# Other waiting times for the recorded mixer streams of a two-layer hybrid decoder

## The chip, the cores and the metric

One core of one Trainium2 chip runs the whole kernel as one program. The metric is the device time of one execution in microseconds (us), lower is better. The kernel before takes 931.92 us, the median of three runs (928.59 to 932.09).

## The reference

The reference is a decoder trunk for one sequence of 256 tokens, 1024 wide, in fp32, with two layers. Cut to what matters:

```python
for layer in range(2):
    h = rms_norm(x, norm1_g[layer])
    w_l = w_in[layer]
    ...
    y_sb = merge_heads(stick_breaking_attention(...))
    y_rwkv, v_first = rwkv7_time_mix(...)
    ...
    y_moba = merge_heads(moba_attention(q_m, k_m, ...))
    y_hgrn = hgrn2_mixer(...)
    merged = None
    for n, y_n in enumerate((y_sb, y_rwkv, y_moba, y_hgrn)):
        gate = jax.nn.sigmoid(cols(GATE_OFF + n * D_MODEL, D_MODEL))
        term = gate * (y_n.astype(x.dtype) @ w_branch[layer, n])
        merged = term if merged is None else merged + term
    x = x + merged @ w_out[layer]
    h2 = rms_norm(x, norm2_g[layer])
    x = x + (jax.nn.silu(h2 @ w_ffn_gate[layer]) * (h2 @ w_ffn_up[layer])) @ w_ffn_down[layer]
return rms_norm(x, final_g)
```

Four token mixers work side by side in a layer. RWKV-7 is a recurrence over the tokens; in layer 1 its value rows are first mixed with those of layer 0, `v + (v_first - v) * sigmoid(v0 + (v @ v1) @ v2)`. MoBA is here plain causal attention with a partial rotary on queries and keys, since its block is as long as the sequence.

## The kernel before, in words

A layer has a mixer phase, a merge and an FFN. In all three the large products run on TensorE (PE) in three passes: every fp32 operand is split into a rounded part `hi` and a rest `lo` (`split`, lines 127 to 129: a CAST on ScalarE, ACT, and a subtraction on VectorE, DVE), and `mm3` multiplies hi by hi, hi by lo and lo by hi. Weights come in pieces of 128x1024 (512 KB) over SP's queue into a ring of four `raw` tiles, and their split into a ring of four `hi`/`lo` pairs (pool tags `spl`): a fifth CAST waits for the last matmul of the first weight.

The mixer phase (`phase`, line 1058) writes two kinds of work into one program. *Units* are the projections, the gates (`gate_unit`) and the branch products (`branch_unit`); they are nearly all of PE's work and are drawn from a list. *Streams* are the mixers' inner parts, written as generators: `rwkv` is one; stick-breaking attention (`sba`), MoBA (`moba`) and HGRN (`hgrn`) follow each other in a second, `rest`. `drive` (line 91) keeps an estimate of PE's time, `pe[0]`. When a stream yields a number, it comes next when the estimate has grown by 1.7 times that number of ns; until then units are written. So the yields set where a stream's pieces stand among the units. Behind that the framework's scheduler orders each engine's list once more by its own estimate of what is ready. Every engine then works through its list strictly in order.

What the prediction's steps touch:

- PSUM tiles: `pa` (three buffers, taken in turn) holds the results of the units, `p1` (two) those of RWKV, `p2` (two) those of the attentions and HGRN, `p3` an attention's output. A gate takes two `pa` tiles (t = 0 and 1, the halves of the sequence); they are free again when ACT has read them through a sigmoid (line 1018). HGRN's last projection takes two; each is read on ACT twice (lines 817 and 818), then on DVE (line 819).
- RWKV's triangular inverse. The 16x16 blocks on the diagonal are inverted on DVE in three levels (lines 598 and 601: products and sums of 2x2, 4x4 and 8x8 sub-blocks). ACT's queue then writes the result `yb` to DRAM (line 606, tile `tri`) and reads it back in another layout (line 609, `cb`); DVE masks it (613) and transposes it (623), and PE grows the inverse to 32, 64 and 128 in steps up to line 686. `pair_scores` (line 540) makes the four score tiles and ends in a masked copy on DVE (548).
- MoBA. The rotary of two tiles is two shuffles (987), four products and sums on DVE (988, 990) and two products on GpSimd, POOL (989). Then for each t: scores on PE, mask on DVE (936), row maximum (997, 998), four exponentials on ACT (1001), their scaling on DVE (1003, 1004), transposes on PE (`flip_att`), weighing with the values. Exponential and sigmoid are in different function tables of ACT, and an ACT_TABLE_LOAD stands where one follows the other.
- HGRN ends with transposes of its output (`y_T`) into a `p2` tile, whose split is the left operand of its two branch products.

Of the kernel before, what the change touches and what calls it, by code (L numbers as in the profile page):

```python
# [46 lines left out]
def trunk(ctx, tc, x, w_t, w_n, w_br, w_out, w_gu, w_dn, par, lora, rows, gains, consts, masks, out):  # L47
# [12 lines left out]
    def ps(tag):  # L60
        return psum.tile([128, 512], F32, name=tag, tag=tag, bufs=NB[tag])
# [409 lines left out]
    def rwkv(m, l, yT):  # L471
# [100 lines left out]
        for c in range(2):  # L572
            LK.append(g2d(sb("b1", 1024), 4))
            pair_scores(kh, LK[c], c)
            yield 2400
        yield 500
        nc.vector.tensor_copy(yb.rearrange("p s t -> p (s t)")[:, 1::34],
                              xb.rearrange("p s t -> p (s t)")[:, 1::34])
        tmp = sb("xy", 512)[0:64]
# [1 line left out]
        for lev in range(1, 4):  # L581
            hb = 1 << lev
            nb = 8 // hb

            def blk(q, i, j):
                return bass.AP(tensor=q.tensor, offset=q.offset + i * hb * 16 + j * hb,
                               ap=[q.ap[0], [34 * hb, nb], [16, hb], [1, hb]])

            pr = tmp[:, 0:nb * hb ** 3].rearrange("p (b i c k) -> p b i c k", b=nb, i=hb, c=hb)
            t4 = th[:, 0:nb * hb * hb].rearrange("p (b i c) -> p b i c", b=nb, i=hb)  # L590
            parts = [(slice(None), i) for i in range(hb)] if hb < nb else [(b, slice(None)) for b in range(nb)]
            bc = [64, nb if hb < nb else hb, hb, hb]

            def product(dst, l4, r4):
                r4 = r4.rearrange("p b k c -> p b c k")
                for b, i in parts:
                    r = r4 if hb < nb else r4[:, b, None]
                    nc.vector.tensor_tensor(pr[:, b, i], l4[:, b, i, None].to_broadcast(bc), r.to_broadcast(bc),
                                            op=OP.mult)
                for b, i in parts:  # L600
                    nc.vector.tensor_reduce(dst[:, b, i], pr[:, b, i], axis=AX.X, op=OP.add)

            product(t4, blk(yb, 0, 0), blk(xb, 0, 1))
            product(blk(yb, 0, 1), t4, blk(yb, 1, 1))
        yield 4000
        nc.scalar.dma_start(tri.rearrange("p (s t) -> p s t", s=16), yb)
        yield 2500
        cb = sb("h1", 256)[:, 0:128].rearrange("p (m t) -> p m t", m=8)
        nc.scalar.dma_start(cb, bass.AP(tensor=tri.tensor, offset=tri.offset, ap=[[16, 128], [2048, 8], [1, 16]]))
        yield 2500  # L610
# [75 lines left out]
                (nc.scalar.copy if u else nc.vector.tensor_copy)(Y[c][L64, u::2, H64], g2d(p[hrow(u), 0:128], 2))  # L686
        yield 900

        if l:
            p = ps("p1")  # L690
            for hp in range(2):
                mm(p[0:64, 0:256], v1[:, hp], vx[:, hp], hp == 0, hp == 1)
            vl = sb("h1", 256)
            nc.scalar.copy(vl[0:64], p[0:64, 0:256])
            yield 1000
            sv = lora_up(v2, vl[0:64], P_V0)
            dv = g2d(sb("c1", 512), 2)
            nc.gpsimd.tensor_tensor(dv, g2d(vfirst, 2), vx, op=OP.subtract)
            nc.gpsimd.tensor_tensor(dv, dv, sv, op=OP.mult)
            nc.gpsimd.tensor_tensor(vx, vx, dv, op=OP.add)  # L700
            yield 6000
        p = ps("p1")
        for c in range(2):
            for hp in range(2):
# [32 lines left out]
        for c in range(2):  # L737
# [55 lines left out]
            nc.vector.tensor_tensor(yc, yc, bonus[:, c], op=OP.add)  # L793
            nc.vector.tensor_tensor(yc, yc, g[:, c], op=OP.mult)
            ys.append(yc)
            yield 200
        yield 6000
        yT[1] = y_T(ys, "p1"), pe[0] + 2500

# [25 lines left out]
    def hgrn(m, l, yT):  # L825
# [79 lines left out]
        for t in range(2):  # L905
# [13 lines left out]
            nc.vector.tensor_tensor(y, y, gs[:, t], op=OP.mult)  # L919
            ys.append(y)  # L920
            yield 300
        yield 3500
        yT[3] = y_T(ys, "p2"), pe[0] + 2500

    def scores(q, k, t, mask):
# [57 lines left out]
    def moba(m, v, yT):  # L983
        r = []
        for u in m:
            o = g2d(sb("c2", 512), 2)
            nc.vector.stream_shuffle(o, g2d(u, 2), SWAP)  # L987
            nc.vector.tensor_tensor(o, o, over(sinT, 2), op=OP.mult)
            nc.gpsimd.tensor_tensor(g2d(u, 2), g2d(u, 2), over(cosT, 2), op=OP.mult)
            nc.vector.tensor_tensor(o, o, g2d(u, 2), op=OP.add)  # L990
            r.append(o)
        yield 5000
        po = ps("p3")
        for t in range(2):
            z, n = scores(r[0], r[1], t, cn[:, K_MO:K_MO + 128])
            mxs = sm.tile([128, 4], F32, name="mxs")
            nc.vector.tensor_reduce(mxs, z, axis=AX.X, op=OP.max)
            nc.vector.tensor_scalar(mxs, mxs, -0.125, None, op0=OP.mult)
            den = sm.tile([128, 4], F32, name="den")
            for a in range(4):  # L1000
                nc.scalar.activation(z[:, a], z[:, a], AF.Exp, bias=mxs[:, a:a + 1], scale=0.125,
                                     accum_out=den[:, a:a + 1])
            nc.vector.reciprocal(den, den)
            nc.vector.tensor_tensor(z, z, bcast(den, n), op=OP.mult)
            yield 5000 + 2500 * t
            ts = []
            flip_att(z, t, ts)
            yield 1200
            weigh(po, ts, t, v, 256)
        yT[2] = y_split(po), pe[0] + 2500  # L1010
        yield 500
# [46 lines left out]
    def phase(hr, g, l, ws):  # L1058
# [32 lines left out]
        def rest():  # L1091
            yield from sba(sm_, vv, yT)
            while len(mm_) < 2:
                yield 2000
            yield from moba(mm_, vv, yT)
            while len(hm) < 4:
                yield 2000
            yield from hgrn(hm, l, yT)
# [202 lines left out]
```

## Time and profile before

| | us |
|---|---|
| median of 3 runs (lowest to highest) | 931.92 (928.59 to 932.09) |
| the profiled execution, its own time | 928.13 |
| its span on the core | 926.3 |
| PE busy | 906.9 (98%) |
| DVE busy | 649.1 (70%) |
| ACT busy | 475.4 (51%) |
| POOL busy | 84.5 (9%) |

The profile is of one execution. Its span runs from the first to the last instruction; around it lie 1.8 us that belong to the execution's own time. Busy times are unions over an engine's instructions. Matmuls overlap, and their ends are modelled, so a row's start is surer than its end. In a timeline a row is a run of equal instructions, with the start, the length, and in brackets the idle time of the engine before it with what ended it. PE's loads of weights are an engine of their own there (PEld).

### The profile page before, as it was taken

What the parts mean: (1) busy time and instruction counts of PE and PEld (TensorE: products, weight loads), DVE (VectorE), ACT (ScalarE), POOL (GpSimd) and SP (SyncE); (2) the same over time, 40 slices, a digit from 0 to 9 for tenths busy, and PEclk for the clock granted to TensorE, in tenths of its full rate; (3) what the DMA queues carried; (4) which work ended last, traced back from release to release, by engine and by line L of the source; (5) the groups of instructions that cost most, each with busy time, mean ns of one, the idle gap of its engine ahead of it and who ended that gap; (6) DMA issues with size and microseconds to landing.
All of it is one profiled execution on the core that took longest, in us unless ns stands there. A gap on an engine that the chain in (4) does not pass through costs nothing.

```text
span 926.3 us, 15024 instructions
## 1 busy us (share of the span) xinstructions
PE 906.9 (98%) x5908; PEld 759.1 (82%) x5908; DVE 649.1 (70%) x958; ACT 475.4 (51%) x727; POOL 84.5 (9%) x94
## 2 busy tenths in 40 slices
PE   8999999999999999999999999999999999999996
PEld 5999677778878888888889986777888888888885
DVE  6668877776766666677567778867678566666665
ACT  5564375355535555456445646644455445545453
POOL 3001100333000000000000201032230000000000
PEclk9999999999999999999999999999999999999999
DMA  8644454345864555568435544444367356556551
GB/s 303 218 151 151 127 163 134 95 154 180 263 210 137 182 184 185 183 205 271 154 114 161 159 140 129 151 117 134 119 215 260 112 185 203 192 180 196 182 182 46
DMA packets 50424, 158.11 MB, mean 171 GB/s; under 512 B 9393, under 2 KB 11953, under 8 KB 50354
## 3 DMA queue, kind: packets, MB, share of 16 engines
q1 hardware_dynamic: 43920, 155.71, 52.7%
q10 hardware_dynamic: 6434, 1.45, 0.7%
q8 instruction: 46, 0.75, 0.3%
q14 instruction: 24, 0.20, 0.1%
HBM read 154.91 MB, written 2.23 MB: 170 GB/s over the span
## 4 chain that ended last, share of the span: by engine, by line
PE 86%; DVE 6%; DMA 3%; issue 2%; ACT 2%; POOL 0%; POOLq 0%; ACTq 0%; SPq 0%; DVEq 0%
PE pa L80 61%; PE p L80 23%; DVE lo L129 1%; PE p L89 1%; PE pa L89 1%; DMA h<-flat 1%; DMA tri<-yb 1%; DMA flat<-b 1%; DMA raw<-in_w_out_dram 1%; DVE b L972 1%; ACT hi L128 0%; DVE b L548 0%; DMA xr<-in_x_dram 0%; DVE c L987 0%; DVE b L874 0%
## 5 line engine op out<-in xcount | busy, mean ns | idle before, releaser
L129 DVE TENSOR_TENSOR lo<-raw,hi 128x1024 fp32r<-128x1024 f32 x268 | 330.2, 1237 | 162.7 <-ACT hi L128 159.9
L128 ACT CAST hi<-raw 128x1024 fp32r<-128x1024 f32 x268 | 279.0, 1048 | 237.8 <-PE pa L80 116.8
L80 PE MATMUL pa<-h,hi 128*128 128x256 f32 (+1 forms) x1280 | 277.9, 339 | 0.0
L80 PEld LDWEIGHTS pa<-h,hi 128*128 128x128 f32 x1280 | 215.9, 190 | 24.6 <-issue 2.0
L80 PE MATMUL pa<-hi,h 128*128 128x512 f32 x576 | 193.5, 400 | 2.2 <-DVE p L819 2.2
L80 PE MATMUL pa<-h,lo 128*128 128x256 f32 x960 | 179.9, 283 | 0.0
L80 PEld LDWEIGHTS pa<-h,lo 128*128 128x128 f32 x960 | 148.6, 191 | 7.0 <-issue 0.7
L80 PEld LDWEIGHTS pa<-hi,h 128*128 128x128 f32 x576 | 108.1, 188 | 27.5 <-DVE p L819 3.0
L80 PE MATMUL p<-hi,c 128*128 128x512 f32 (+1 forms) x352 | 113.4, 394 | 0.0
L80 PE MATMUL pa<-lo,h 128*128 128x512 f32 x288 | 112.6, 391 | 0.0
L80 PEld LDWEIGHTS p<-hi,c 128*128 128x128 f32 x352 | 66.1, 189 | 15.2 <-DVE c L129 0.6
L80 PE MATMUL p<-lo,c 128*128 128x512 f32 (+1 forms) x176 | 69.2, 393 | 0.0
L80 PEld LDWEIGHTS pa<-lo,h 128*128 128x128 f32 x288 | 54.2, 188 | 10.1 <-issue 0.3
L263 POOL TENSOR_TENSOR rs<-rs,half 128x1 f32<-128x1 f32 x10 | 6.2, 618 | 477.3 <-DVE rs L262 477.3
L80 PE MATMUL pa<-hi,y 128*128 128x512 f32 x128 | 43.9, 399 | 0.0
L80 PE MATMUL p<-hi,b 128*128 128x512 f32 x128 | 41.5, 397 | 0.6 <-DVE b L129 0.6
L80 PEld LDWEIGHTS p<-lo,c 128*128 128x128 f32 x176 | 33.2, 188 | 6.8
L1040 POOL TENSOR_TENSOR p<-p,gt 128x512 f32<-128x512 f32 x16 | 31.2, 1975 | 54.4 <-DVE gt L1038 54.4
L342 DVE TENSOR_TENSOR gt<-gt,pa 128x256 f32<-128x256 f32 x80 | 33.2, 415 | 0.0
L128 ACT CAST c<-xy 128x512 fp32r<-128x512 f32 x20 | 12.4, 620 | 39.2 <-DVE xy L1143 39.2
L80 PEld LDWEIGHTS pa<-hi,y 128*128 128x128 f32 x128 | 24.0, 188 | 6.4 <-issue 1.0
L341 ACT COPY gt<-pa 128x256 f32<-128x256 f32 x80 | 29.2, 366 | 0.0
(277 smaller groups left out, 939.6 us busy)
## 6 DMA issues: line engine op xcount, KB each, us to landing
raw<-in_w_gu_dram SPq DMA_DIRECT2D x88, 512.0 KB, 3.9
raw<-in_w_n_dram SPq DMA_DIRECT2D x80, 512.0 KB, 3.6
raw<-in_w_dn_dram SPq DMA_DIRECT2D x44, 512.0 KB, 3.6
raw<-in_w_t_dram SPq DMA_DIRECT2D x40, 512.0 KB, 4.1
raw<-in_w_br_dram SPq DMA_DIRECT2D x16, 512.0 KB, 3.6
raw<-in_w_out_dram SPq DMA_DIRECT2D x16, 512.0 KB, 4.4
b<-in_gains_dram SPq DMA_DIRECT2D x4, 512.0 KB, 5.6
flat<-b ACTq DMA_DIRECT2D x4, 256.0 KB, 3.2
```

The costliest lines, as they stand in the source:

```text
L80: nc.tensor.matmul(o, l, r, start=start, stop=stop)
L89: nc.tensor.transpose(o, i, ident)
L128: a = nc.scalar.copy(dst[0], src)
L129: return a, (eng or nc.vector).tensor_tensor(dst[1], src, dst[0], op=OP.subtract)
L263: nc.gpsimd.tensor_tensor(dst, dst, half[:, :dst.shape[-1]], op=OP.pow)
L341: nc.scalar.copy(dst, p[:, 256:512])
L342: nc.vector.tensor_tensor(dst, dst, p[:, 0:256], op=OP.add)
L972: nc.vector.tensor_tensor_scan(kb, kb, reset[t][:, ::-1], 1.0, op0=OP.mult, op1=OP.add)
L1040: e.tensor_tensor(mg[f, t], mg[f, t], g, op=OP.add)
```

## The change

All edits are in the yields and in the order in which the generators issue their work; no operation is added or taken away. (a) Behind the scores of RWKV's second kind the yields become 3000 and 3000 instead of 2400, 2400 and 500. (b) The inverse's three levels yield 100 behind each of their six products, and 1200 behind the last instead of 4000. (c) In layer 1 the mixing of the value rows (two low-rank products on PE, a copy and two sigmoids on ACT, three operations on POOL) is issued between the write of `tri` and its read, instead of behind the whole inverse; in layer 0 a yield of 1000 stands there. (d) The yields behind RWKV's two output halves are 1500 and 200 instead of 200 twice, behind HGRN 4300 instead of 3500, behind MoBA's two softmaxes 6800 and 8300 instead of 5000 and 7500. (e) 5000 more stand ahead of MoBA.

```diff
--- before.py
+++ after.py
@@ -572,8 +572,7 @@
         for c in range(2):
             LK.append(g2d(sb("b1", 1024), 4))
             pair_scores(kh, LK[c], c)
-            yield 2400
-        yield 500
+            yield 3000
         nc.vector.tensor_copy(yb.rearrange("p s t -> p (s t)")[:, 1::34],
                               xb.rearrange("p s t -> p (s t)")[:, 1::34])
         tmp = sb("xy", 512)[0:64]
@@ -601,10 +600,26 @@
                     nc.vector.tensor_reduce(dst[:, b, i], pr[:, b, i], axis=AX.X, op=OP.add)
 
             product(t4, blk(yb, 0, 0), blk(xb, 0, 1))
+            yield 100
             product(blk(yb, 0, 1), t4, blk(yb, 1, 1))
-        yield 4000
+            yield 100
+        yield 1200
         nc.scalar.dma_start(tri.rearrange("p (s t) -> p s t", s=16), yb)
-        yield 2500
+        if l:
+            p = ps("p1")
+            for hp in range(2):
+                mm(p[0:64, 0:256], v1[:, hp], vx[:, hp], hp == 0, hp == 1)
+            vl = sb("h1", 256)
+            nc.scalar.copy(vl[0:64], p[0:64, 0:256])
+            yield 1000
+            sv = lora_up(v2, vl[0:64], P_V0)
+            dv = g2d(sb("c1", 512), 2)
+            nc.gpsimd.tensor_tensor(dv, g2d(vfirst, 2), vx, op=OP.subtract)
+            nc.gpsimd.tensor_tensor(dv, dv, sv, op=OP.mult)
+            nc.gpsimd.tensor_tensor(vx, vx, dv, op=OP.add)
+        else:
+            yield 1000
+        yield 1500
         cb = sb("h1", 256)[:, 0:128].rearrange("p (m t) -> p m t", m=8)
         nc.scalar.dma_start(cb, bass.AP(tensor=tri.tensor, offset=tri.offset, ap=[[16, 128], [2048, 8], [1, 16]]))
         yield 2500
@@ -686,19 +701,6 @@
                 (nc.scalar.copy if u else nc.vector.tensor_copy)(Y[c][L64, u::2, H64], g2d(p[hrow(u), 0:128], 2))
         yield 900
 
-        if l:
-            p = ps("p1")
-            for hp in range(2):
-                mm(p[0:64, 0:256], v1[:, hp], vx[:, hp], hp == 0, hp == 1)
-            vl = sb("h1", 256)
-            nc.scalar.copy(vl[0:64], p[0:64, 0:256])
-            yield 1000
-            sv = lora_up(v2, vl[0:64], P_V0)
-            dv = g2d(sb("c1", 512), 2)
-            nc.gpsimd.tensor_tensor(dv, g2d(vfirst, 2), vx, op=OP.subtract)
-            nc.gpsimd.tensor_tensor(dv, dv, sv, op=OP.mult)
-            nc.gpsimd.tensor_tensor(vx, vx, dv, op=OP.add)
-            yield 6000
         p = ps("p1")
         for c in range(2):
             for hp in range(2):
@@ -793,7 +795,7 @@
             nc.vector.tensor_tensor(yc, yc, bonus[:, c], op=OP.add)
             nc.vector.tensor_tensor(yc, yc, g[:, c], op=OP.mult)
             ys.append(yc)
-            yield 200
+            yield 1500 - 1300 * c
         yield 6000
         yT[1] = y_T(ys, "p1"), pe[0] + 2500
 
@@ -919,7 +921,7 @@
             nc.vector.tensor_tensor(y, y, gs[:, t], op=OP.mult)
             ys.append(y)
             yield 300
-        yield 3500
+        yield 4300
         yT[3] = y_T(ys, "p2"), pe[0] + 2500
 
     def scores(q, k, t, mask):
@@ -1002,7 +1004,7 @@
                                      accum_out=den[:, a:a + 1])
             nc.vector.reciprocal(den, den)
             nc.vector.tensor_tensor(z, z, bcast(den, n), op=OP.mult)
-            yield 5000 + 2500 * t
+            yield 6800 + 1500 * t
             ts = []
             flip_att(z, t, ts)
             yield 1200
@@ -1092,6 +1094,7 @@
             yield from sba(sm_, vv, yT)
             while len(mm_) < 2:
                 yield 2000
+            yield 5000
             yield from moba(mm_, vv, yT)
             while len(hm) < 4:
                 yield 2000
```

What the scheduler makes of it shows in the engines' lists. First DVE in layer 0, around the last level of the inverse: `yb` is the inverse, `xy_1232` or `xy_1235` its products, `c2_1161` or `c2_1226` a rotary tile of MoBA, `lo_` the split of weights, `b1_1178` or `b1_1174` the last score tile of RWKV. Before:

```order
L988 TENSOR_TENSOR c2_1161<-c2_1161,cn_70 128x512
L601 TENSOR_REDUCE yb_124<-xy_1232 64x4x4
L990 TENSOR_TENSOR c2_1161<-c2_1161,p_920 128x512
L601 TENSOR_REDUCE yb_124<-xy_1232 64x4x4
L129 TENSOR_TENSOR lo_1289<-raw_1286,hi_1288 128x1024
L548 COPY_PREDICATED b1_1178<-mk_122,p1_1179 128x2x256
L548 COPY_PREDICATED b1_1178<-mk_122,p1_1180 128x2x256
L598 TENSOR_TENSOR xy_1232<-yb_124,h1_1126 64x512
L601 TENSOR_REDUCE h1_1233<-xy_1232 64x64
L598 TENSOR_TENSOR xy_1232<-h1_1233,yb_124 64x512
L129 TENSOR_TENSOR lo_1307<-raw_1304,hi_1306 128x1024
L601 TENSOR_REDUCE yb_124<-xy_1232 64x8x8
```

Of the change:

```order
L990 TENSOR_TENSOR c2_1226<-c2_1226,cn_70 128x512
L600 TENSOR_REDUCE yb_124<-xy_1235 64x4x4
L992 TENSOR_TENSOR c2_1226<-c2_1226,p_920 128x512
L129 TENSOR_TENSOR lo_1257<-raw_1254,hi_1256 128x1024
L600 TENSOR_REDUCE yb_124<-xy_1235 64x4x4
L597 TENSOR_TENSOR xy_1235<-yb_124,h1_1126 64x512
L548 COPY_PREDICATED b1_1174<-mk_122,p1_1175 128x2x256
L548 COPY_PREDICATED b1_1174<-mk_122,p1_1176 128x2x256
L600 TENSOR_REDUCE h1_1236<-xy_1235 64x64
L597 TENSOR_TENSOR xy_1235<-h1_1236,yb_124 64x512
L129 TENSOR_TENSOR lo_1287<-raw_1284,hi_1286 128x1024
L600 TENSOR_REDUCE yb_124<-xy_1235 64x8x8
```

The rotary's last rows (988 and 990 before, 990 and 992 now) stand in both ahead of the 8x8 level; two masked copies and one split have changed places with their neighbours, and the instructions down to the inverse's last sum are the same.

Next ACT in layer 0, at the first gate behind HGRN's projections: `pa_1284` and `pa_1285` before, `pa_1252` and `pa_1253` now are the gate's two results, `c2_1255` or `c2_1322` MoBA's scores for t = 0, `tri_958` the inverse in DRAM. Before:

```order
L128 CAST hi_1350<-raw_1348 128x1024
L1001 ACT_TABLE_LOAD
L1001 ACTIVATE c2_1255,den_1267<-c2_1255,mxs_1264 128x128 x4
L128 CAST hi_1399<-raw_1397 128x1024
L128 CAST hi_1429<-raw_1427 128x1024
L128 CAST hi_1451<-raw_1449 128x1024
L945 COPY c2_1346<-p2_1341 128x512
L1018 ACT_TABLE_LOAD
L1018 ACTIVATE gt_1360<-pa_1284 128x512
L1018 ACTIVATE gt_1370<-pa_1285 128x512
```

Of the change:

```order
L128 CAST hi_1343<-raw_1341 128x1024
L624 DMA h1_1358<-tri_958 128x8x16
L128 CAST hi_1367<-raw_1365 128x1024
L128 CAST hi_1393<-raw_1391 128x1024
L128 CAST hi_1415<-raw_1413 128x1024
L1020 ACTIVATE gt_1353<-pa_1252 128x512
L1003 ACT_TABLE_LOAD
L1003 ACTIVATE c2_1322,den_1334<-c2_1322,mxs_1331 128x128 x4
L1020 ACT_TABLE_LOAD
L1020 ACTIVATE gt_1363<-pa_1253 128x512
L128 CAST hi_1437<-raw_1435 128x1024
```

The four exponentials and their two table loads stood ahead of both gate sigmoids; now they stand between the first and the second. The read of `tri` has moved behind a CAST (before it stood ahead of line 817 for t = 1).

Last PE in layer 0, at the transposes of HGRN's output (`p2_2354` or `p2_2457`); their split is `y_2359` and `y_2360` before, `y_2462` and `y_2463` now. Before:

```order
L89 MATMUL p2_2354<-cn_70,h2_2269 128x128
L89 MATMUL p2_2354<-cn_70,h2_2298 128x128
L89 MATMUL p2_2354<-cn_70,h2_2269 128x128
L89 MATMUL p2_2354<-cn_70,h2_2298 128x128
L80 MATMUL pa_2238<-hi_2339,h4_140 128x512
L80 MATMUL pa_2238<-lo_2340,h4_140 128x512
L80 MATMUL pa_2238<-hi_2339,h4_140 128x512
L80 MATMUL pa_2368<-hi_2372,h4_139 128x512
L80 MATMUL pa_2368<-lo_2373,h4_139 128x512
L80 MATMUL pa_2368<-hi_2372,h4_139 128x512 x2
```

Of the change:

```order
L80 MATMUL pa_2311<-hi_2417,h4_140 128x512
L89 MATMUL p2_2457<-cn_70,h2_2377 128x128
L89 MATMUL p2_2457<-cn_70,h2_2406 128x128
L89 MATMUL p2_2457<-cn_70,h2_2377 128x128
L89 MATMUL p2_2457<-cn_70,h2_2406 128x128
L80 MATMUL pa_2472<-hi_2468,y_2462 128x512
L80 MATMUL pa_2472<-lo_2469,y_2462 128x512
L80 MATMUL pa_2481<-hi_2468,y_2462 128x512
L80 MATMUL pa_2481<-lo_2469,y_2462 128x512
L80 MATMUL pa_2472<-hi_2468,y_2463 128x512
L80 MATMUL pa_2472<-hi_2468,y_2462 128x512
L80 MATMUL pa_2472<-lo_2469,y_2462 128x512
```

Behind the transposes followed the rest of one gate and a whole further gate before the branch products with `y_2359`; now the branch products with `y_2462` follow at once. Layer 1 reads the same at this place.

## Rows read from the trace of the kernel before

**Rows 1.** The page: PE's line of part 1 (busy us, share of the span, instructions), and the granted clock of the 40 slices of part 2 in tenths.

```profile
PE 906.9 (98%) x5908; PEld 759.1 (82%) x5908; DVE 649.1 (70%) x958; ACT 475.4 (51%) x727; POOL 84.5 (9%) x94
...
PEclk9999999999999999999999999999999999999999
```

**Rows 2.** The waits of PE over the whole span: engine, tile and line that waited, what for; us in total, times, longest.

```profile
PE p L89 <- DVE c L1004: 2.5, 2, 1.3
PE pa L80 <- DVE p L819: 2.2, 2, 1.1
PE p L80 <- DVE b L548: 1.6, 2, 0.8
...
PE p L80 <- DVE h L767: 1.0, 1, 1.0
```

**Rows 3.** The timeline of PE in layer 0's mixer phase: start us, us, engine, line, operation, out<-in, shapes, count, and in brackets the idle time before and what ended it. From the row at 111.98 to the idle time ahead of the one at 120.39 PE works off thirty matmuls of 512 columns.

```profile
93.30 1.13 PE L80 MATMUL p<-b,c 64*128 64x256 f32 x8
...
99.22 1.75 PE L80 MATMUL p<-b,c 64*128 64x256 f32 x8 [0.77 <-DVE b L548]
...
107.24 0.71 PE L80 MATMUL p<-c,c 64*128 64x128 f32 x8
107.88 0.50 PE L80 MATMUL pa<-hi,h 128*128 128x512 f32 x1
...
111.98 0.50 PE L80 MATMUL pa<-hi,h 128*128 128x512 f32 x1 [1.07 <-DVE p L819]
...
120.39 0.63 PE L89 MATMUL p<-cn,c 128*128 128x128 f32 x4 [1.32 <-DVE c L1004]
```

**Rows 4.** The timeline of DVE over the same stretch.

```profile
97.19 0.72 DVE L987 STREAM_SHUFFLE c<-p 128x512 f32<-128x512 f32 x1
...
98.46 1.32 DVE L548 COPY_PREDICATED b<-mk,p 128x512 f32<-128x512 uint8 x2
...
108.44 1.20 DVE L129 TENSOR_TENSOR lo<-raw,hi 128x1024 fp32r<-128x1024 f32 x1
109.58 0.67 DVE L601 TENSOR_REDUCE yb<-xy 64x64 f32<-64x512 f32 x1
...
111.50 0.42 DVE L819 TENSOR_TENSOR p<-p,pa 128x256 f32<-128x256 f32 x1
111.84 0.75 DVE L936 TENSOR_TENSOR c<-p,cn 128x256 f32<-128x256 f32 x2
112.62 0.69 DVE L997 TENSOR_REDUCE mxs<-c 128x4 f32<-128x512 f32 x1
113.34 0.17 DVE L998 TENSOR_SCALAR mxs<-mxs 128x4 f32<-128x4 f32 x1
...
116.97 1.28 DVE L613 TENSOR_TENSOR xy<-h,mk 128x512 f32<-128x512 f32 x2
118.17 1.29 DVE L623 STREAM_TRANSPOSE xy<-xy 128x512 f32<-128x512 f32 x2
```

**Rows 5.** The timeline of ACT over the same stretch; ACTq is its queue, on which it issues DMAs.

```profile
110.28 0.49 ACTq L606 DMA_DIRECT2D tri<-yb  x1
110.81 0.37 ACT L817 COPY p<-pa 128x256 f32<-128x256 f32 x1 [3.77 <-DVE yb L601]
111.08 0.39 ACT L818 ACTIVATE p<-pa 128x256 f32<-128x256 f32 x1
113.61 0.38 ACTq L609 DMA_DIRECT2D h<-tri  x1
...
115.64 1.28 ACT L1001 ACT_TABLE_LOAD   x1
116.94 0.40 ACT L1001 ACTIVATE c<-c,mxs 128x128 f32<-128x128 f32 x1
...
118.50 2.93 ACT L128 CAST hi<-raw 128x1024 fp32r<-128x1024 f32 x3
```

**Rows 6.** The DMAs that write or read `tri`, all four of them: from issue to landing.

```profile
DMA to landing us min/median/max: 2.8/2.9/3.3
```

**Rows 7.** Groups of ACT by line with forms kept apart: count, busy us, mean ns of one, idle time before.

```profile
L1018 ACT ACTIVATE gt<-pa 128x512 f32<-128x512 f32 x32 | 18.5, 596 | 8.7 <-PE pa L80 8.4
...
L1001 ACT ACTIVATE b<-b,mxs 128x256 f32<-128x256 f32 x8 | 4.0, 498 | 0.0
```

**Rows 8.** The timeline of layer 0 behind the scores for t = 1: DVE's maximum and scaling of MoBA, and PE's 32-wide step of the inverse.

```profile
127.78 1.21 DVE L997 TENSOR_REDUCE mxs<-b 128x4 f32<-128x1024 f32 x1
...
133.36 1.22 DVE L1004 TENSOR_TENSOR b<-b,den 128x1024 f32<-128x1024 f32 x1
...
145.36 0.69 PE L80 MATMUL p<-h,b 32*32 32x32 f32 x32
```

**Rows 9.** The timeline at the end of layer 0's HGRN: its transposes on PE and the split of their result on ACT and DVE.

```profile
208.25 0.60 PE L89 MATMUL p<-cn,h 128*128 128x128 f32 x4
...
208.88 0.59 ACT L128 CAST y<-p 128x512 fp32r<-128x512 f32 x1 [0.46 <-PE p L89]
...
209.50 0.69 DVE L129 TENSOR_TENSOR y<-p,y 128x512 fp32r<-128x512 f32 x1 [0.79 <-ACT y L128]
```

**Rows 10.** The timeline of PE in layer 1, at the two places that answer to 111.98 and 120.39 in layer 0.

```profile
565.75 0.50 PE L80 MATMUL pa<-hi,h 128*128 128x512 f32 x1 [1.09 <-DVE p L819]
...
574.00 0.63 PE L89 MATMUL p<-cn,c 128*128 128x128 f32 x4 [1.16 <-DVE c L1004]
```

## The prediction

> **What bounds the kernel now.** I read the page first: PE is busy for 98% of the span and the granted clock is at its upper level, 2.4 GHz, in every slice [rows 1]. So other engines cost time only where they let PE wait, and the change leaves PE's work as it is. The table of PE's waits comes next: the mixer phases of both layers lose 2.5 us to the scaling of MoBA's probabilities, 2.2 us to HGRN's line 819, 1.6 us to RWKV's masked copy and 1.0 us to line 767 [rows 2]. The timeline shows where: one stall each in either layer, and for the copy more than the idle time says, because the same eight matmuls take 1.13 us at 93.30 and 1.75 us at 99.22, a hidden 0.62 us [rows 3]. What could be won by moving instructions is thus about 7.3 + 1.2 = 8.5 us, 0.9%; the question is which stalls go and what is late next. The orders of the engines say more on this than the yields do.
>
> **The inverse and the stall at line 819.** PE needs HGRN's first result buffer back at 111.98. It comes back when DVE ends line 819 at 111.92, which started at 111.50, and that waited for ACT's lines 817 and 818 at 110.81 and 111.08 [rows 3 to 5]. ACT was late because the write of `tri` stands ahead of them in its queue and was issued at 110.28 only, right behind the inverse's last sum (109.58 + 0.67 = 110.25) [rows 4, 5]. In the changed order ACT's write of `tri` still stands ahead of both evictions, and DVE has the same instructions ahead of that last sum: the rotary was not moved out of the inverse. So the buffer is free at 111.98 again.
>
> What PE does until then is another matter. Six more matmuls now stand ahead of the last pair of RWKV's score products. At (120.39 - 1.32 - 111.98) / 30 = 0.236 us each [rows 3] they bring it to 99.22 - 0.77 + 1.42 = 99.87 us, while the second copy ends at 98.46 + 1.32 = 99.78 [rows 4]: the stall at 548 goes, 0.77 + 0.62 = 1.39 us. But MoBA's scores for t = 0, 107.88 - 107.24 = 0.64 us [rows 3], now stand behind the gate. PE reaches the buffer with 1.39 us less waiting and 0.64 us less work done, and waits there 1.07 + 1.39 + 0.64 = 3.1 us. Nothing is won, and the 0.64 us of scores are still to be done: +0.64 us a layer.
>
> **Layer 0, the first gate.** From 111.98 PE has 30 matmuls (7.1 us), the scores (0.64), 12 matmuls of the gate and 12 of a branch product (2.8 each) to work off, until 125.4; then it needs the buffer that the gate's second sigmoid frees. In ACT's new order that sigmoid stands behind MoBA's four exponentials and a table load, and the exponentials wait for the row maximum on DVE. DVE comes to it late: it first needs the inverse read back, whose issue can't be earlier than the landing of `tri`, 113.61, and which lands 2.9 us later [rows 5, 6], at 116.5. Then follow, in DVE's order, by start-to-start steps of [rows 4]: two maskings (0.60 each) and two transposes (0.61), three weight splits (109.58 - 108.44 = 1.14), two score masks (0.78 together), the maximum (0.72) and its scaling (0.17): 7.5 us, so 124.0. The four exponentials take 118.50 - 116.94 = 1.56 us, the table load 1.28 us [rows 5], the sigmoid 0.60 [rows 7]: 127.5. PE waits 127.5 - 125.4 = 2.1 us.
>
> A rule of the Trainium skill speaks of this step. The trace shows 116.94 - 115.64 = 1.30 us from a load's start to the next instruction [rows 5]. "ScalarE: Activation LUTs", section "What ACT_TABLE_LOAD costs", counts a drain of about 1.38 us on top of a load of about 1.28 us for every switch. By the page each of the three waits reckoned here and below would be some 1.4 us longer, an estimate of 4 us in all; the row shows no such gap, so I go by the row.
>
> The same happens for t = 1. From 127.5 PE has 42 gate matmuls until the next gate's first result is done (9.9 us), with a flip, weighing, scores and two inverse steps between them, 0.4 to 1.1 us each by their like in [rows 3], estimated at 4.3 us together, then 18 matmuls (4.2): it needs the next gate's second buffer at 145.9. The scores end at 140.0; masks (0.8), one inverse copy (0.4, as the equally large line 819 [rows 4]), the wider maximum (1.2) [rows 8] and its scaling lead to 142.7; ACT's first sigmoid and a load end at 143.7, then four exponentials (0.498 each, 2.0 [rows 7]), the second load and the second sigmoid: 147.6. PE waits 1.7 us. I cost both with what hides them subtracted; with an exponential group 2 us earlier either is nothing, 2 us later it is twice as much.
>
> In return the stall at MoBA's flip goes, 1.32 us [rows 3]: now 33 gate matmuls lie between the scaling and the flip. The stall at 767 goes too, 1.0 us [rows 2], because nine more matmuls stand between the state's product and its use. Layer 0 so far: 0.64 + 2.1 + 1.7 - 1.32 - 1.0 = +2.1 us.
>
> **Layer 1** runs like layer 0 up to its own buffer wait at 565.75 [rows 10]: +0.64. Here the value mixing stands in PE's and ACT's order ahead of the exponentials. Its matmuls are moved, not added; they fill PE by about 2 us, and the two gate sigmoids come behind the exponentials together, just when PE asks for the first buffer: 0. Its POOL work is off PE's chain. For t = 1 the flip stands early: behind the last weight CAST that the ring holds back, ACT has that CAST (1.05, by 2.93 for three), a load (1.28) and the exponentials (2.0) [rows 5, 7], then DVE the scaling (1.22 [rows 8]) and its reciprocal (0.2, as line 998 [rows 4]): 5.7 us, while PE has 18 matmuls (4.2) and a 32-wide step (0.7 [rows 8]): +0.8 us. The flip stall of 1.16 us [rows 10] goes. Together 0.64 + 0.8 - 1.16 = +0.3 us.
>
> **The end of HGRN, both layers.** The transposes were covered by more than a gate's matmuls; now the branch product with their result follows at once. PE has the transposes' result at 208.25 + 0.60, ACT ends the CAST at 209.47, and DVE's rest at 210.19 covers itself by the four matmuls that use the CAST alone [rows 9]. Were PE to go on behind the transposes (from 208.6 by four steps of about 0.1), it would stand until 209.5: 0.9 us. ACT first has the gate's second sigmoid to end (+0.1). I take 0.9 us a layer; the lower end is 0.5 (the CAST alone), the upper 2.1 (both halves and a second sigmoid in front). Sum +1.8 us.
>
> **Sum.** 2.1 + 0.3 + 1.8 = +4.2 us. Against the profiled execution's 928.13 us that is 932.3, +0.45%. The median of the runs, 931.92, lies 3.8 us above that execution, within their scatter; the forecast for the median is 931.92 + 4.2 = 936.1 us. About 0.5% (4.7 us) is what a measurement of this kernel can tell from no change.
>
> **The rivals.**
> 1. *The exponentials don't hold the gates.* If the row maximum comes some 2 us earlier than I count, the waits of 2.1, 1.7 and 0.8 us vanish: 4.2 - 4.6 = -0.4, 931.5 us. For it: DVE waits for the inverse read back while three splits stand behind it, and I count that wait whole. Against: the 113.61 us is a landing, not an issue in DVE's hands.
> 2. *The inverse does end earlier* (faster). If the rotary's five DVE rows left the chain, from 0.6 us for a shuffle upwards [rows 4] some 3.3 us together, the write of `tri` would go out at 107 and line 819 stall PE no more: the 1.07 and 1.39 us of either layer are won, the scores still paid, and the read comes earlier too, which takes away rival 1's 4.6. That is 4.2 - 2 x (1.07 + 1.39) - 4.6 = -5.3, 926.6 us. It decides once the last sum is 3.1 us earlier. For it: the yields ask for it. Against: DVE's order, which has the rotary where it was.
> 3. *The ends grow.* If HGRN's normalisation is not done when PE comes to the transposes, or the loads drain as the page says, each layer loses another 2 us: 940 us. A stall of 3.1 us is also longer than any in the rows, the longest in the phases being 1.32 us at an undisturbed 2.4 GHz [rows 1, 3]; a clock halved for as long as the stall would cost 1.6 us each time, 939 us.
>
> The Trainium skill, "TensorE: Matmul & The Clock Gate", section "Loop structure matters more than you think", warns that a wait inside the loops can drop the clock; no row here shows a drop at such a wait, and I leave it inside rival 3.
>
> **How the numbers follow.** The forecast gets 0.50, with its own range 932 to 940 (each of the four waits is good to 0.7 us, and the scatter of the runs is 3.5); rival 1 gets 0.22, rival 2 0.13, rival 3 0.15. Above 936.6 us lie 0.23 of the forecast and rival 3: 0.39 with 0.01 of rival 1. Below 927.3 lie 0.10 of rival 2 and 0.02 of rival 1: 0.12. The rest, 0.49, is no change that can be told. The range 927.5 to 941 leaves out about one in ten on either side.
>
> **What the changed profile would show.** PE's waits: line 548 gone, the wait for line 819 (821 now) at about 3 us in either layer with its end still just behind the write of `tri`; MoBA's scaling gone from the list in layer 0; new waits of PE's large products for ACT's gate sigmoid (1020), two in layer 0; a wait of PE for the CAST or the split of `y` behind HGRN's transposes in both layers, some 0.9 us. The forecast is wrong if the write of `tri` is issued well before 110 us, if no gate sigmoid appears among PE's releasers, or if PE's idle time in the phases falls below 8 us.

## The result, and the profile after

The changed kernel takes 937.53 us, the median of 4 runs (936.66 to 941.1), against 930.39 us (4 runs, 928.59 to 932.09) for the kernel before: ratio 1.0086, 95% interval 1.0063 to 1.0108. It is slower by about 7 us; the forecast was 936.1 us in a range of 927.5 to 941. The profiled execution took 936.82 us with a span of 935.0 us, 8.7 us more than before. PE works 3.5 us longer (910.4 against 906.9 [rows 1]) and stands the rest. Of the runs below one of e7's (990.94 us) was in a slower state: the ratios leave it out, e7's median holds it (929.67 us without it).

PE's waits in the changed kernel (what waited, for what; us in total, times, longest):

```profile
PE pa L80 <- DVE p L821: 6.6, 2, 3.3
PE pa L80 <- ACT gt L1020: 1.8, 2, 1.4
...
PE p L89 <- DVE b L1006: 1.4, 1, 1.4
PE pa L80 <- ACT y L128: 1.4, 2, 0.7
PE p L89 <- DVE h L921: 0.9, 2, 0.8
PE pa L80 <- DVE p L1038: 0.9, 1, 0.9
PE p L80 <- DVE c L877: 0.8, 2, 0.5
```

Of [rows 2] the waits for 548 and 767 are gone, and so are the 2.5 us for MoBA's scaling of t = 0 (tile `c`); that of t = 1 (tile `b`) is waited for instead, 1.4 us, in layer 1 alone. HGRN's line 819, now 821, grew from 2.2 to 6.6 us. Gates (1020; 1038, DVE's product of a gate and a branch result), HGRN's 877 and its transposes (921, and the CAST of `y`) are new. Where they stand on PE's timeline, layer 0 above, layer 1 below:

```profile
112.09 0.50 PE L80 MATMUL pa<-hi,h 128*128 128x512 f32 x1 [3.32 <-DVE p L821]
126.41 0.50 PE L80 MATMUL pa<-hi,h 128*128 128x512 f32 x1 [0.92 <-DVE p L1038]
129.41 0.50 PE L80 MATMUL pa<-hi,h 128*128 128x512 f32 x1 [0.43 <-ACT gt L1020]
221.96 0.50 PE L80 MATMUL pa<-hi,y 128*128 128x512 f32 x1 [0.68 <-ACT y L128]
464.86 0.63 PE L89 MATMUL pa<-cn,b 128*128 128x128 f32 x4 [0.46 <-DVE b L284]
566.61 0.50 PE L80 MATMUL pa<-hi,h 128*128 128x512 f32 x1 [3.27 <-DVE p L821]
604.77 0.63 PE L89 MATMUL p<-cn,b 128*128 128x128 f32 x4 [1.40 <-DVE b L1006]
668.93 0.50 PE L80 MATMUL pa<-hi,h 128*128 128x512 f32 x1 [1.38 <-ACT gt L1020]
682.72 0.55 PE L89 MATMUL p<-cn,h 128*128 128x128 f32 x3 [0.78 <-DVE h L921]
683.94 0.50 PE L80 MATMUL pa<-hi,y 128*128 128x512 f32 x1 [0.68 <-ACT y L128]
```

The row at 464.86 is the wait at layer 0's end that the kernel before has at 463.85. So up to there 1.0 us are lost, 0.2 of it in the start, and layer 1 lost the other 7.7. The waits for 1006 and for the gate at 668.93 have no like in layer 0, and 682.72 has one of 0.17 us only. The wait of 3.27 us had a second price in layer 1. Here are stretches behind it (PE busy, count, granted clock, DMA share, GB/s):

```profile
566.00:568.00 2.00, 1.39 (x6) 1.00 0.75 256
568.00:570.00 2.00, 2.00 (x7) 0.50 0.75 246
570.00:572.00 2.00, 2.00 (x8) 0.65 0.79 252
572.00:574.00 2.00, 2.00 (x10) 1.00 0.71 213
```

The clock fell to 0.50, 1.2 GHz. Three products of 512 columns in a row take 0.69 us from start to start on either side; there they took 1.17, 1.28 and 1.20 us: 1.6 us lost. In layer 0 the clock stayed up behind a wait just as long.

### The profile page after: what moved, and what is told of

Read it like the earlier page. It is cut to its first block, busy times and chain, and to the rows that moved or that the text cites. A ratio compares the mean times of both kernels' runs of the same rounds, so it can differ in the third digit from the quotient of the medians.

```text
span 935.0 us, 15023 instructions
## 1 busy us (share of the span) xinstructions
PE 910.4 (97%) x5908; PEld 762.3 (82%) x5908; DVE 649.7 (69%) x958; ACT 477.1 (51%) x727; POOL 81.5 (9%) x94
## 5 line engine op out<-in xcount | busy, mean ns | idle before, releaser
L1042 POOL TENSOR_TENSOR p<-p,gt 128x512 f32<-128x512 f32 x16 | 27.7, 1750 | 107.9 <-DVE gt L1040 69.9
```

Of the source, the lines that this page charges most:

```text
L1042: e.tensor_tensor(mg[f, t], mg[f, t], g, op=OP.add)
```

## The experiments

I compare each run's trace with that of before by the starts of the same matmul of PE's list: one ahead of all edits (about 99 us), one in layer 0's FFN, one in layer 1's. The differences are what each layer costs. It is needed because the start, where PE's list is the same in all kernels, differs by up to 3.3 us between the traces, and the runs of one kernel spread as far (28 runs of before: 927.3 to 932.0). The ratios are to runs of before taken together with each kernel. Whether the clock fell in a layer moves its figure too: in layer 0 the changed kernel and e4 have the same list on PE and stand at +0.8 and +1.8.

| kernel | median us | ratio to before, 95% | start | layer 0 | layer 1 | clock fell in mixers of layer |
|---|---|---|---|---|---|---|
| changed | 937.53 | 1.0086 (1.0063 to 1.0108) | +0.2 | +0.8 | +7.7 | 1 |
| e1 | 939.1 | 1.0092 (1.0067 to 1.0116) | +3.3 | +1.7 | +8.7 | 0, 1 |
| e2 | 939.67 | 1.0088 (1.0066 to 1.011) | +3.3 | +1.5 | +7.9 | 0, 1 |
| e3 | 935.3 | 1.0052 (1.0033 to 1.007) | +3.2 | +0.5 | +5.6 | 1 |
| e4 | 933.63 | 1.0041 (1.0025 to 1.0058) | +0.3 | +1.8 | +3.4 | 0, 1 |
| e5 | 934.09 | 1.0057 (1.0041 to 1.0073) | -0.1 | +2.6 | +2.2 | 0, 1 |
| e6 | 930.67 | 1.0008 (0.9994 to 1.0022) | +3.2 | -1.6 | 0.0 | 0 |
| e7 | 930.73 | 1.0009 (0.9992 to 1.0026) | 0.0 | -0.8 | +1.1 | none |
| e8 | 933.46 | 1.0035 (1.0019 to 1.0052) | +0.3 | +1.0 | +0.9 | 0 |
| e9 | 932.79 | 1.0025 (1.0006 to 1.0044) | -0.1 | +1.7 | +1.8 | 0, 1 |
| e10 | 927.14 | 0.9958 (0.9938 to 0.9978) | 0.0 | -2.1 | +1.2 | 1 |
| e11 | 930.65 | 1.0002 (0.9985 to 1.0019) | +3.2 | -1.7 | +1.0 | 0 |
| e12 | 939.19 | 1.0082 (1.0064 to 1.01) | +3.2 | +4.2 | +4.1 | 0, 1 |

**Who holds PE at line 821: e1, e2, e3.** Three kernels, edits one by one and together:

```diff
-        nc.scalar.dma_start(tri.rearrange("p (s t) -> p s t", s=16), yb)
+        nc.gpsimd.dma_start(tri.rearrange("p (s t) -> p s t", s=16), yb)
```

> The changed kernel with one word changed: the write of the inverse to `tri` is issued from GpSimd's queue, not from ScalarE's; the order on TensorE and VectorE stays as it is. ScalarE then isn't held at that write until 110.4 us. Theory Q (the forecast's own: the evictions L819 and L820 are late because ScalarE stands at the write, in order): TensorE's wait behind L821 falls from 3.3 to about 1.1 us in both layers, and the half clock behind it in layer 1 goes too (1.7 us): 937.5 - 2.2 - 2.2 - 1.7 = 931.4. Theory V (VectorE decides: L821 reads PSUM itself and stands on VectorE behind the last pieces of the inverse, L600 at 109.7 and the `lo` of L129 at 110.3, so it can't start before 111.5 however early ScalarE is): the wait stays 3.2 us, 937.3. Both together would give something between only if L821 moved.

```diff
-            nc.vector.tensor_tensor(gs[:, t], gs[:, t], p[:, 256:512], op=OP.mult)
+            raw = sb("h2", 256)
+            nc.scalar.copy(raw, p[:, 256:512])
+            nc.vector.tensor_tensor(gs[:, t], gs[:, t], raw, op=OP.mult)
```

> The changed kernel in which ScalarE copies the gate half out of PSUM and VectorE multiplies from that copy, so that TensorE waits for ScalarE alone at this place; the write of `tri` stays on ScalarE's queue. Theory Q (ScalarE's queue): nothing is won, two copies of 0.4 us are added behind 110.9, TensorE resumes at about 112.3 instead of 112.1: 937.5 to 938. Theory V (VectorE): if VectorE alone held it, TensorE would go on behind ScalarE's first copies, and about 2 us a layer and the half clock would be won: 931 to 932.

> Both edits together: `tri` written from GpSimd's queue, and VectorE out of the way. If the wait has two causes side by side (ScalarE's queue to 110.4, VectorE's to 111.5), only this one takes it away: wait 0.7 to 1.1 us in each layer, no half clock, 937.5 - 2.3 - 2.3 - 1.7 = 931.2. Theory Q alone: same as the first of these runs, 931.4. Theory V alone: same as the second, 931 to 932. If TensorE is then stopped by something else in the same place (the third `pa` tile, weights), the wait stays over 2 us and the time over 935.

Neither edit alone won anything. In e1 ACT is freed early and DVE is not (rows of the timeline in layer 0; this execution's start was 3.3 us later than before's):

```profile
109.20 0.37 ACT L819 COPY p<-pa 128x256 f32<-128x256 f32 x1 [0.30 <-PE pa L80]
...
112.83 0.67 DVE L600 TENSOR_REDUCE yb<-xy 64x64 f32<-64x512 f32 x1
113.43 1.20 DVE L129 TENSOR_TENSOR lo<-raw,hi 128x1024 fp32r<-128x1024 f32 x1
114.56 0.73 DVE L821 TENSOR_TENSOR p<-p,pa 128x256 f32<-128x256 f32 x2
...
115.01 0.50 PE L80 MATMUL pa<-hi,h 128*128 128x512 f32 x1 [3.13 <-DVE p L821]
```

ACT reads the buffer at 109.20, as soon as PE has it done, yet DVE's 821 stands in order behind the inverse's last sum and a weight split. In e2, where DVE no longer reads the buffer, PE waits as long (6.2 us in the two layers) for ACT's copy. So two engines held PE side by side. With both out of the way (e3) the wait at 821 is gone, and the time falls by 0.34% of before, not by the 0.7% expected. PE stands 13 us later instead:

```profile
128.41 0.50 PE L80 MATMUL pa<-hi,h 128*128 128x512 f32 x1 [3.42 <-DVE p L1040]
```

PE waits there for the buffer of a branch product, which DVE gives back with 1040, behind MoBA's maximum; DVE had waited for the inverse read back. In the changed kernel this wait was 0.92 us.

**Layer 1's value mixing: e4, e5, e7.** In e4 the mixing goes back behind the inverse, all else stays changed. With it comes back the yield of 6000 that stood behind it and that change (c) dropped; the two were not tried apart, and "the mixing's place" below means both:

```diff
         nc.scalar.dma_start(tri.rearrange("p (s t) -> p s t", s=16), yb)
-        if l:
-            ...
-        else:
-            yield 1000
+        yield 1000
         yield 1500
...
+        if l:
+            ...
+            yield 6000
         p = ps("p1")
```

> The changed kernel with layer 1's value mixing back at its old place (behind the inverse's products); the cut inverse and all other waits of the change stay. Layer 1 lost 7.7 us and layer 0 only 1.0. Theory M (the mixing in its new place, its two matmul groups, evictions and the sigmoid of L483 with its table load beside MoBA's exponentials, delays layer 1's MoBA: 1.5 us behind the scaling L1006 and 1.5 us behind the gates' sigmoids, against 0.9 and 0.4 in layer 0): layer 1 comes down to layer 0's waits, 937.5 - 2 to - 3 = 934.5 to 935.5. Rival (the half clock and the ends of HGRN make the difference, the mixing is hidden either way): 936.5 to 938.5.

3.9 us by the medians, 4.3 us by layer 1 of the table, somewhat over what was expected. PE's waits in e4 show what went: the waits for 1006 (1.4) and for the gate at 668.93 (1.4) are not in them, and that for HGRN's 921 is down to the one in layer 0:

```profile
PE pa L80 <- DVE p L821: 6.6, 2, 3.3
...
PE pa L80 <- DVE p L1038: 0.9, 1, 0.9
PE p L89 <- DVE h L921: 0.5, 1, 0.5
...
PE pa L80 <- ACT gt L1020: 0.4, 1, 0.4
```

One way it acts can be read off ACT's queue. In the changed kernel, layer 1:

```profile
564.93 0.47 ACTq L607 DMA_DIRECT2D tri<-yb  x1
...
574.35 0.37 ACT L613 COPY h<-p 64x256 f32<-64x256 f32 x1 [0.61 <-PE p L80]
574.35 0.38 ACTq L624 DMA_DIRECT2D h<-tri  x1
```

And in e4:

```profile
566.03 0.47 ACTq L607 DMA_DIRECT2D tri<-yb  x1
...
570.21 0.41 ACTq L611 DMA_DIRECT2D h<-tri  x1
```

The read of `tri` now stands behind the mixing's eviction 613, which waits 0.61 us for PE, and behind a CAST that waits 3.17 us for PE (at 572.69). It goes out 9.4 us behind the write instead of 4.2 (layer 0: 113.68 - 110.39 = 3.3). It also takes less time to land, 2.2 us against 5.3 in e4, so the inverse is back 11.6 us behind the write instead of 9.4, 2.2 us later. That this delay makes the three waits is not shown. For the gate at 668.93 the trace of the changed kernel shows something else on ACT:

```profile
666.17 0.62 ACT L128 CAST c<-raw 128x512 fp32r<-128x512 f32 x1 [3.60 <-DMA raw<-in_w_gu_dram]
...
668.28 0.60 ACT L1020 ACTIVATE gt<-pa 128x512 f32<-128x512 f32 x1
```

The sigmoid stands behind the CASTs of the FFN's first weights, and ACT had waited 3.60 us for one of these to land. In e4 the like wait is 0.88 us (at 664.90). So part of what e4 wins can be the order in which later work meets the weights.

e5 joins e4 with the two edits of e3:

```diff
-        nc.scalar.dma_start(tri.rearrange("p (s t) -> p s t", s=16), yb)
+        nc.gpsimd.dma_start(tri.rearrange("p (s t) -> p s t", s=16), yb)
...
+            nc.scalar.copy(raw, p[:, 256:512])
```

> The changed kernel with three of the edits tried so far at once: `tri` written from GpSimd's queue, the gate half copied by ScalarE, and layer 1's value mixing back at its old place. If the two causes found add up (3.9 us for the mixing's place, 2.2 us for the wait behind L821): 937.5 - 3.9 - 2.2 = 931.4, which is the time of before (930.4 to 931.0). Rival: with both edits the 3.4 us wait of layer 0 came back 14 us later, behind the branch product's input (DVE, first gates); with the mixing back layer 1 then has layer 0's order and shows that wait too, so that the edits win nothing but the half clock: 933 to 934.

The rival was right in kind, and the time is just above its range: PE waits 8.0 us for 1040 in the two layers, and nothing is won over e4.

e7 is the kernel before with the mixing alone moved up (and its yield of 6000 gone):

```diff
         nc.scalar.dma_start(tri.rearrange("p (s t) -> p s t", s=16), yb)
+        if l:
+            ...
+        else:
+            yield 1000
-        yield 2500
+        yield 1500
...
-        if l:
-            ...
-            yield 6000
         p = ps("p1")
```

> The kernel before with one part of the change alone: layer 1's value mixing moved up behind the write of `tri`. Theory A (its place costs by itself: two matmul groups, an eviction and a sigmoid with its table load where ScalarE and VectorE are busiest): what its way back won comes here as a loss, 930.9 + 3.9 = 934.8. Rival B (it costs only together with the MoBA that is held back, since there its sigmoid falls beside the exponentials and the inverse's second half): 930.0 to 932.0. Rival C (alone it helps, since the 20 us of layer 1 behind the inverse get shorter): under 930.

B: no difference that can be told (1.0009); by its trace layer 1 loses 1.1 us. The mixing's place costs in the changed kernel, where MoBA is held back, and little without the other edits.

**The wait ahead of MoBA: e6, e10, e11.**

```diff
-            yield 5000
             yield from moba(mm_, vv, yT)
```

> The changed kernel without the one wait that stands ahead of MoBA (all other edits stay, the value mixing's new place too): MoBA's first scores come 42 products of the projection earlier and stand ahead of the gate projection's end again, and gates stand behind HGRN's last transposes. By the forecast's terms: the wait behind L548 comes back (1.4 and 1.0 us), the wait behind L821 falls from 3.3 to about 1.1 in both layers (-4.4), the half clock of layer 1 goes (-1.7), the ends of HGRN lose 0.9 a layer (-1.8): 937.5 + 2.4 - 4.4 - 1.7 - 1.8 = 932.0. Rival (the holding back is not what costs; the mixing's place and MoBA's later flips are): 936 to 938.

Taking this one line back undoes nearly all of the loss: 930.67 us, 1.0008 of before, with the mixing still in its new place. By the traces it is worth more, since e6's start was a late one: +8.5 us of the two layers against -1.7. The wait at 821 shrank to 2.4, not to 1.1 us, but almost nothing else is left:

```profile
PE pa L80 <- DVE p L821: 4.8, 2, 2.4
...
PE pa L80 <- DVE gt L1040: 0.7, 1, 0.7
```

No wait for 1006, for `y` or for 921. The wait for 548 that was expected back did not come back. What the hold moves shows on DVE in layer 0. In the changed kernel MoBA's maximum (999) stands behind the first use of the inverse read back (628):

```profile
118.42 0.69 DVE L628 TENSOR_TENSOR xy<-h,mk 128x512 f32<-128x512 f32 x1 [3.78 <-DMA h<-tri]
...
124.88 0.67 DVE L999 TENSOR_REDUCE mxs<-c 128x4 f32<-128x512 f32 x1
```

In e6 it stands ahead of it:

```profile
115.85 0.69 DVE L999 TENSOR_REDUCE mxs<-c 128x4 f32<-128x512 f32 x1
...
120.82 1.28 DVE L628 TENSOR_TENSOR xy<-h,mk 128x512 f32<-128x512 f32 x2
```

The kernel before with the hold alone was not run, so whether the hold costs as much without the other edits stays open.

e10 takes back the hold and the mixing's place:

```diff
-            yield 5000
             yield from moba(mm_, vv, yT)
...
-        if l:
-            ...
-        else:
-            yield 1000
+        yield 1000
```

> The changed kernel without the wait ahead of MoBA and with layer 1's value mixing back at its old place. With the hold the mixing's place was worth 3.9 us, alone in the kernel before 0 (930.7 against 929.9). If it costs only beside a MoBA that is held back, this comes out as without the hold: 929.5 to 931.5. If its new place helps the inverse's readers where MoBA is early, 932 or more. If it costs in any case: 927 to 928.5.

927.14 us, 0.9958 of before (interval under 1): the lowest median of the study, below before's and e6's, and in the range of the third case. By the medians the mixing would cost 3.5 us here too. The traces don't bear that out: behind the start e6 stands at -1.7 and e10 at -0.9 against before, and e6's profile began 3.2 us late. Most of the distance between e6 and e10 can be the start; twelve and ten runs don't settle it.

e11 takes back the hold and MoBA's later flips:

```diff
-            yield 5000
             yield from moba(mm_, vv, yT)
...
-            yield 6800 + 1500 * t
+            yield 5000 + 2500 * t
```

> The changed kernel without the wait ahead of MoBA and with MoBA's own waits behind the exponentials as before (5000 + 2500 t in place of 6800 + 1500 t). By the forecast the later flips take the wait for the scaled scores away (1.32 us in layer 0, 1.16 in layer 1, behind L1004 before): they come back here, 930.7 + 2.5 = 933.2. Rival: the wait for the flip is hidden by the wait behind L821 that stands ahead of it: 930 to 931.5.

930.65 us, the rival: without the hold the later flips bring nothing that the medians can tell.

**Can the inverse's round trip be taken off PE: e8, e9, e12.** e8 is the kernel before and e9 is e6, both with the two edits of e3; e12 is e10 with them and with the read of `tri` moved as well:

```diff
-        nc.scalar.dma_start(tri.rearrange("p (s t) -> p s t", s=16), yb)
+        nc.gpsimd.dma_start(tri.rearrange("p (s t) -> p s t", s=16), yb)
...
+            nc.scalar.copy(raw, p[:, 256:512])
...
-        nc.scalar.dma_start(cb, bass.AP(tensor=tri.tensor, ...
+        nc.gpsimd.dma_start(cb, bass.AP(tensor=tri.tensor, ...
```

> The kernel before with the two edits that together took the wait behind L821 out of the changed kernel: `tri` written from GpSimd's queue, the gate half of the projection copied out of PSUM by ScalarE. In the kernel before that place costs TensorE 1.07 and 1.09 us (rows of L819), so up to 2.2 us are to be won: 928.7 if they go, with nothing late behind them. Rival: the place behind it (second half of the gates, 1.32 and 1.16 us behind L1004) grows by as much: 930.5 to 931.5.

> The changed kernel without the wait ahead of MoBA, and with both edits at the gate projection's end (`tri` written from GpSimd's queue, the gate half copied by ScalarE). Without the hold TensorE still stood 2.4 us behind L821 in each layer, its only long wait in the mixers. If nothing is late behind it, now that the scores stand ahead: 930.7 - 2 x 2.4, and 1.7 for the half clock that followed in layer 0 = 924.2 to 926, faster than the kernel before. Rival: as in the two kernels before it the wait comes back at the next input that VectorE makes behind the inverse (the scaled scores L1008 or the branch product L1040): 930 to 932.

> The best variant so far (no wait ahead of MoBA, value mixing at its old place) with ScalarE's queue cleared altogether: the write and also the read of `tri` are issued from GpSimd's queue, and the gate half is copied by ScalarE. In the variant with the write alone moved, ScalarE stood 8.3 us at the read, which waits for the write to land, with casts of weights behind it, and TensorE then waited 3.7 and 2.6 us for ScalarE. If that in-order queue is the last cause, the 2.5 us behind L821 go in both layers and the half clock with them (1.7): 927.1 - 4.9 - 1.7 = 920.5 to 923. Rival: TensorE is stopped next by the first thing that VectorE makes behind the inverse (scaled scores L1008, the product L1040), as in every such edit before: 926 to 930.

All three are slower than the kernels they start from, e9 clearly so only by its layers (its interval overlaps e6's), and all three lie above the ranges of their rivals too. In e8 the wait comes back at MoBA's scaling (5.1 us in the two layers, against 2.5 [rows 2]). In e9 ACT stands at the read of `tri`, with the casts of weights behind it:

```profile
114.80 0.37 ACTq L624 DMA_DIRECT2D h<-tri  x1
115.21 0.37 ACT L819 COPY p<-pa 128x256 f32<-128x256 f32 x1 [8.30 <-DMA tri<-yb]
...
120.08 0.50 PE L80 MATMUL pa<-hi,h 128*128 128x512 f32 x1 [3.74 <-ACT hi L128]
```

In e12 ACT is clear, and DVE stands at the same round trip, with the splits of the weights behind it:

```profile
121.77 1.29 DVE L615 TENSOR_TENSOR xy<-h,mk 128x512 f32<-128x512 f32 x2 [4.82 <-DMA h<-tri]
...
126.25 0.80 PE L80 MATMUL pa<-lo,h 128*128 128x512 f32 x1 [5.11 <-DVE lo L129]
```

In each of these kernels an engine that PE's weights pass through stood at the DMA to DRAM and back, with the next weights in order behind it. No variant tried here keeps all of them clear.

## Why the prediction was right or wrong

The total was right, and partly by luck: 936.1 us forecast, 937.53 measured, but the forecast stood on 931.92 us for before, where four runs give 930.39, and its change of +4.2 us met +7.1 by the medians and +8.7 in the profiled spans. Its parts were right less often. They gave layer 0 +3.0 us (2.1 and 0.9 for HGRN's end) and layer 1 +1.2; the traces give +0.8 and +7.7.

- *The wait at line 821* was right in place and size: 3.1 us forecast, 3.32 and 3.27 measured, and the wait for 548 went. Its reason was half of the truth: e1 shows that DVE holds the buffer as long as ACT does.
- *Layer 0's first gate*, 2.1 us forecast. It took 0.92 + 0.43 us. PE ran out of buffers at 126.41 - 0.92 = 125.49, as forecast (125.4), but the buffer it needed there was one that DVE's 1038 gives back, which also stands behind the maximum; that of the second sigmoid it needed only at 128.98. The chain came later as well: the maximum's scaling ended at 125.76 (forecast 124.0) and the second sigmoid at 129.36 (127.5). The read of `tri` went out as forecast, at 113.68, but landed 4.7 us later, not 2.9. That the sum comes near the forecast is luck: two errors work against each other.
- *Layer 0's second gate*, 1.7 us forecast: none. The sigmoid's time was right (147.49 + 0.60 = 148.1 against 147.6), the place at which PE asks for its buffer was not: PE works without a break from 140.68 until behind the sigmoid's end. This term was mis-sized by all of itself.
- *The flip and 767* went as forecast in layer 0, -2.3 us. A wait of 0.55 us for a split in its merge (at 256.15 before) went too, and one of 0.52 us for 877 (at 199.00) came, both unforeseen.
- *HGRN's end*, 0.9 us a layer: 0.68 us for the CAST of `y`, the mechanism named, and with it 0.17 us in layer 0 and 0.78 in layer 1 for the late input 921, which had been put in rival 3.
- *Layer 1* holds the step that failed: "Its matmuls are moved, not added; they fill PE by about 2 us, and the two gate sigmoids come behind the exponentials together, just when PE asks for the first buffer: 0." At its own place this held: PE waits for neither of these two sigmoids. What failed is that the mixing's new place was given no price behind that: 4.3 us by e4. The flip for t = 1 took 1.40 us (0.8 forecast, by the mechanism named), a later gate 1.38 and HGRN's transposes 0.78 us (both 0), and e4 takes all three away, while the first gates' 0.86 and 0.41 us come back.
- *Rival 3's clock* came in layer 1, 1.6 us, the price reckoned. The Trainium skill, "TensorE: Matmul & The Clock Gate", section "Loop structure matters more than you think", has a long DMA wait between matmuls turn TensorE cold; here the wait was for VectorE, and the trace agrees in layer 1 and not in layer 0.
- *Rival 3's longer table loads* did not come: from a load's start to the next sigmoid's it is again 1.30 us (127.46 to 128.76).
- *Rival 2* stayed out: the write of `tri` went out at 110.39 us, against 110.28 [rows 5].

Layer 1's waits, with one of 0.31 us for 877 beside those shown, sum to 7.8 us, against 3.3 in before (1.09 and 1.16 [rows 10], 0.83 for 548, 0.20 for 746): 4.5 of the 7.7 us. The other 3.2 us are products that take longer from start to start with the waits left out: 1.2 in the units' products of 512 columns (the clock's 1.6, less what others won) and 2.0 in the streams' small ones, above all those of 64 columns (0.8) and the transposes (0.7). The forecast had no term for the small products, and why they take longer stays open.

## What to carry to other kernels

When two streams share in-order engines, holding one back does not take it out of the other's way: here it moved the one's reads behind the other's round trip, and beside the other edits that one line cost some 7 us. Before a queue is blamed for a wait, look for a second engine that would end as late; free both in one run, and read from the next wait whether anything was won. Work moved ahead of a DMA's issue delays it by what the work waits for, not by what it takes: a copy of 0.37 us and a CAST put the read 5.2 us back. Then see when the DMA lands; here that was 2.2 us later.

## What the runs showed of the hardware

The granted clock fell to 0.50 behind most of the longer waits in the mixers, but a wait's length doesn't decide it: it fell behind 3.27 us in layer 1 of the changed kernel and not behind 3.32 us in its layer 0, behind 2.4 us in layer 0 of e6 and not behind as much in its layer 1, and in e3 behind 1.61 us in layer 1 and not behind 3.42 us in layer 0. Behind the waits in the mixers of the kernel before, up to 1.32 us, it never fell.

The same DMA does not always take the same time: the read of `tri` landed 2.2 us after its issue in both layers of e9 and 6.4 us after it in layer 1 of e3.

The start has two forms in the fourteen traces, late in e1, e2, e3, e6, e11 and e12 and early in the others, though PE's list is the same there. PE's same first products, in before and then in e6:

```profile
4.76 1.36 PE L199 MATMUL p<-b,h 1*128 1x512 f32 x2
```

```profile
4.77 2.07 PE L199 MATMUL p<-b,h 1*128 1x512 f32 x2
```

They go on at the lower rate in e6 until it is 3.2 us behind. The first record of the granted clock, at 1.00, begins 12.6 to 14.1 us into the six late traces and 4.3 to 5.3 us into the eight early ones; what was granted ahead of it is not on record. A difference under about 3 us between medians of a few runs should be read with the traces beside it.
